# Hyena filters interleaved with the S5 tables in a two-layer hybrid backbone

## The chip, the cores and the metric

The kernel runs on one core of one Trainium2 chip. The metric is device time in microseconds (us), the median of three runs. A core has a matrix engine (TensorE, PE in the rows), a vector engine (VectorE, DVE), a scalar engine (ScalarE, ACT), a general engine (GpSimd, POOL) and a queue engine (SyncE, SP) that here issues nearly all transfers. Each engine works through its own instructions in order; semaphores tie them together.

## The reference, cut to what matters

Two layers act on 256 latent tokens and 256 context tokens. Layer 0, the one concerned, mixes tokens in three parallel branches read from one input projection:

```python
p = modulate(x, shift, scale) @ w_in                  # (L, 6656)
# Hyena: filters are functions of position, then two gated long convolutions
h = sin(freq0 * (z @ w1 + b1)); h = sin(freq1 * (h @ w2 + b2))
h = (h @ w3 + b3) * exp(-tn * abs(decay))             # filters, (L, 2 orders, 2 directions, 512)
z = parts[-1]
for o in range(2):
    z = parts[o] * two_sided_long_conv(z, h[:, o, 0], h[:, o, 1], bias[o])   # by FFT
# Conformer: GLU, depthwise convolution of 31 taps, LayerNorm, swish
# S5: diagonal state space of 64 states in 32 groups of 16 channels, both directions
abar = exp(lam * dt); bbar = (abar - 1) / lam * b
y = Re(C scan(abar, bbar u)) ; y = g * sigmoid(g @ w_glu), g = gelu(y + d * u)
out = (sig(g_hy) * y_hy + sig(g_cf) * y_cf + sig(g_s5) * y_s5) @ w_o
```

A feed-forward network follows, dense in layer 0 and with eight experts in layer 1. Everything is float32.

## The kernel before, in words

A float32 matmul is done as three with the operands split into a high and a low part (`mm3`, L119 to L123); ScalarE casts the high part and VectorE subtracts the low one (`split`, L113 and L114). Weights come as `land` tiles of 128x1024 from the queue SP and are split the same way. The input projection `p` runs in 128x512 tiles.

What depends on the parameters alone is worked out on the chip before it is used, and written as tables to device memory.

- `s5_pre(l)` makes the S5 tables. It has a head (exponentials and sines of all groups) and then four blocks of eight groups. Per block: load `bc`; small products `bb` (L255 to L260); two tiles `cb` made by GpSimd (L265, L268); complex products on VectorE (`cmul`, L277 to L282, tiles `sw` and `tm`); matmuls `kp` (L292, L295), their copy `kt`, the transposes `kq`, the copy `kf`, to which `kd` is added (L306); 15 transfers of `kf` to the table `s5kk` (L309); 16 transposes `tp`, copies `weT` and their transfers (L316 to L318); the same products again on GpSimd (`s5wc`); and sines of the step angles (`tr`, L328 and after).
- `hy_filters(l)` makes the spectra of the long convolutions' filters. Two sine stages (`hp`, L493 and L495; `hid`, L498), then for each of two orders: four tiles `h`, each a matmul times a window `win`, an exponential from ScalarE (L514 to L518); sums and differences `hs` (L526), split into `hh` and `hl`; the transform `kh` of 12 matmuls; its copy `ko` (L534) and the transfer to the table `kd` (L535).

The mixer then uses these: `hy_kk` loads the spectra as `kk` (L609) into the ring "K"; `zc` and `zs` are the forward transforms, products with `kk` follow on VectorE (L581 to L586), `iv` are the inverse ones. `s5_main` has per block `ep`, `yp` (tables `we`, `tb`, `wc`, `mt`), the sum `ya` (L422) and its transposes `yt` (L427). `gl` is the S5 branch's gate, `dc` the conformer's convolution, with taps at L671, a mean taken off at L677 and the variance `va` at L684; `bo` are the branches' output projections.

Tiles live in rings: a ring has a fixed number of buffers under one tag, and its next tile waits for the release of the oldest. The ring of `u2` has four buffers and takes tiles of 128x512; here pass `bc`, `bb`, `cb`, `kf`, `kt` and `kd` of S5 and `win`, `hs` and `ko` of the filters. Ring "K" (taken by `t4(..., "K")`) has two.

The order of instructions on each engine is made when the program is built: a scheduler orders them from the order of the program, priorities, dependences and rings. `self.bg` is a list of generators that `pump` drains, one after the other; in layer 0 first all of `s5_pre(0)`, then all of `hy_filters(0)` (L1458). `both(a, bs)` is a generator that advances `a` one step and then `bs` two.

Of the kernel before, what the change touches and what calls it, by code (L numbers as in the profile page):

```python
# [80 lines left out]
class Net:  # L81
# [392 lines left out]
    def hy_filters(self, l):  # L474

        nc = self.nc
        zT = self.t2([33, 256], "zT")
        nc.sync.dma_start(zT, self.i["zT"])
        w12 = self.t2([64, 2, 64], "w12")
        nc.sync.dma_start(w12[0:33, 0], self.i["hy_f_w1"][l])  # L480
        nc.sync.dma_start(w12[:, 1], self.i["hy_f_w2"][l])
        hc = self.sm.tile([128, 6], FT, name="hc", tag="hc", bufs=1)
        nc.sync.dma_start(hc[0:64, 0:4], self.i["hyc"][l])
        nc.sync.dma_start(hc[:, 4:6], self.i["tn"])
        dft = self.hy_table(self.mx, "dft", tag="U", bufs=self.bufs["U"])
        hid = self.t2([65, 256], "hid")
        ag = self.t2([64, 512], "ag")
        nc.vector.memset(hid[64:65], 1.0)
        a, nn = ag[:, :256], ag[:, 256:]
        for q in range(2):  # L490
            pp = self.ps("hp", "aux")[0:64, 0:256]
            if q == 0:
                nc.tensor.matmul(pp, w12[0:33, 0], zT, start=True, stop=True)  # L493
            else:
                nc.tensor.matmul(pp, w12[:, 1], hid[0:64], start=True, stop=True)  # L495
            nc.vector.tensor_scalar(a, pp, hc[0:64, q:q + 1], hc[0:64, 2 + q:3 + q], op0=OP.add, op1=OP.mult)
            self.reduce2pi(a, nn, (P1, P2, P3))
            nc.scalar.activation(hid[0:64], a, AF.Sin)  # L498
        yield
        for o in range(2):  # L500
            w3 = self.t4([65, 1024], "w3", "U")
            nc.sync.dma_start(w3, self.i["hy_w3a"][l, :, o * 1024:(o + 1) * 1024])
            dec = self.t4([128, 1024], "dec", "U")
            nc.sync.dma_start(dec, self.i["hy_decay"][l:l + 1, o * 1024:(o + 1) * 1024].to_broadcast([128, 1024]))
            nc.vector.scalar_tensor_tensor(dec, dec, -1.0, dec, op0=OP.mult, op1=OP.max)
            bias = self.t2([1, 512], "bias")
            nc.sync.dma_start(bias, self.i["hy_bias"][l, o:o + 1])
            hq = []
            for q in range(2):
                h = self.t4([128, 2, 512], "h", "Y")  # L510
                hq.append(h)
                for tt in range(2):
                    win = self.u2([128, 512], "win")
                    nc.scalar.activation(win, dec[:, q * 512:(q + 1) * 512], AF.Exp, scale=hc[:, 4 + tt:5 + tt])  # L514
                    pp = self.ps("h3", "aux")
                    nc.tensor.matmul(pp, hid[:, tt * 128:(tt + 1) * 128], w3[:, q * 512:(q + 1) * 512],
                                     start=True, stop=True)
                    nc.vector.tensor_mul(h[:, tt], pp, win)  # L518
                yield
            nc.vector.tensor_add(hq[0][0:1, 0], hq[0][0:1, 0], bias)  # L520
            nc.vector.memset(hq[1][0:1, 0], 0.0)
            for r in range(2):
                hh, hl = (self.t4([128, 2, 512], n, "Y", FR) for n in ("hh", "hl"))
                for tt in range(2):
                    hs = self.u2([128, 512], "hs")
                    nc.vector.tensor_tensor(hs, hq[0][:, tt], hq[1][:, tt], op=OP.add if r == 0 else OP.subtract)  # L526
                    self.split(hh[:, tt], hl[:, tt], hs)
                for ft in range(2):
                    ko = self.u2([128, 512], "ko")
                    pp = self.ps("kh", "aux")  # L530
                    c = slice(r * 256 + ft * 128, r * 256 + ft * 128 + 128)
                    for tt in range(2):
                        self.mm3(pp, [t[:, tt, c] for t in dft], (hh[:, tt], hl[:, tt]), tt == 0, tt == 1)
                    nc.scalar.activation(ko, pp, AF.Copy, scale=1.0 / 256.0)  # L534
                    nc.sync.dma_start(self.kd[l][o, r, :, ft], ko)  # L535
                yield
# [867 lines left out]
    def body(self, dbg=None):  # L1404
# [44 lines left out]
        with tc.high_priority():  # L1449
# [5 lines left out]
            for g in m:  # L1455
                self.run(g)
            self.prepare(xr, (0, 1), self.mo[0, 0], self.mo[0, 1])
        self.bg = [self.s5_pre(0), self.hy_filters(0)]  # L1458
        self.pump(1000)
        self.dfs = self.hy_table(self.dftp, "dfs")  # L1460

# [116 lines left out]
```

## Time and profile before

| | |
|---|---|
| runs | 2612.32, 2604.16, 2600.77 us; median 2604.16 |
| profiled execution | 2605.18 us, of it the span of the profile 2603.3 |
| TensorE (matmul) | 2361.7 us busy, 91% |
| VectorE | 2157.8 us, 83% |
| ScalarE | 1373.9 us, 53% |
| GpSimd | 191.6 us, 7% |
| transfers | 229 GB/s over the span |
| mean granted clock of TensorE | 0.943 of full speed |

TensorE is the busiest engine, and most of the span belongs to the feed-forward parts and the experts. The change lies in layer 0's token mixer, roughly the first 500 us. So the page's sums say little; the rows below cut that stretch into windows and then follow single engines through it. In a row of the timeline an instruction's start and duration are followed by engine, line, operation and tiles; in square brackets stands how long the engine had been idle before and what ended that.

### The profile page before, as it was taken

The page shows a single profiled execution, that of the slowest core. Times are in us where ns is not written, and L with a number is a line of the kernel's source. Part 1 is how long each engine was busy: PE and PEld are TensorE (multiplying, and loading weights), DVE is VectorE, ACT ScalarE, POOL GpSimd, SP SyncE. Part 2 cuts the span into 40 slices and gives each one's busy share as a digit, 9 for nine tenths or more (in the row PEclk, how much of TensorE's full clock was granted, in tenths as well). Part 3 has the DMA queues.
Part 4 walks back from the last instruction along what each step waited for, and adds up shares of the span by engine and source line. Part 5 has one row for each costly group of instructions (what it writes and reads, how often), then busy time and mean ns, then how long its engine had stood idle before and what let it go on. Part 6 is the DMA issues. An engine that isn't in the chain of part 4 may idle for free. (4 is left out here: it accounts for less than half of the span.)

```text
span 2603.3 us, 35249 instructions
## 1 busy us (share of the span) xinstructions
PE 2361.7 (91%) x12456; PEld 1935.8 (74%) x12456; DVE 2157.8 (83%) x3182; ACT 1373.9 (53%) x1957; POOL 191.6 (7%) x210
## 2 busy tenths in 40 slices
PE   7958989999899999968869969999999999999986
PEld 2735876788788778748759958888887788878775
DVE  7877899974758988875798678888988889888897
ACT  3434432333543323325435537777877777777775
POOL 1540010000100023230000010000000000000000
PEclk8968999999899999989879979999999999999998
DMA  6546425542235555655535539989999898999985
GB/s 240 190 166 146 137 90 170 194 155 91 80 107 179 182 177 185 208 212 160 162 94 155 178 125 360 347 326 353 352 357 348 324 346 334 354 352 354 351 314 221
DMA packets 170713, 597.26 MB, mean 229 GB/s; under 512 B 59606, under 2 KB 68504, under 8 KB 127520
## 3 DMA queue, kind: packets, MB, share of 16 engines
q1 hardware_dynamic: 170528, 594.94, 65.1%
q8 instruction: 99, 1.62, 0.2%
q14 instruction: 86, 0.70, 0.1%
HBM read 561.87 MB, written 33.00 MB: 229 GB/s over the span
## 5 line engine op out<-in xcount | busy, mean ns | idle before, releaser
L114 DVE TENSOR_TENSOR mwl<-mland,mwh 128x1024 fp32r<-128x1024 f32 x672 | 788.2, 1219 | 78.0 <-ACT mwh L113 65.0
L113 ACT CAST mwh<-mland 128x1024 fp32r<-128x1024 f32 x672 | 675.9, 1052 | 126.9 <-PE mp L123 37.3
L113 ACT CAST wh<-land 128x512 fp32r<-128x512 f32 x396 | 244.9, 621 | 516.0 <-PE p L122 210.7
L114 DVE TENSOR_TENSOR wl<-land,wh 128x512 fp32r<-128x512 f32 x396 | 293.8, 746 | 122.8 <-ACT wh L113 115.6
L123 PE MATMUL p<-hh,wl 128*128 128x256 f32 (+1 forms) x800 | 271.9, 343 | 3.0 <-DVE wl L114 2.9
L121 PE MATMUL p<-hh,wh 128*128 128x256 f32 (+1 forms) x800 | 271.4, 340 | 2.4 <-DVE w L583 1.4
L122 PE MATMUL p<-hl,wh 128*128 128x256 f32 (+1 forms) x800 | 269.9, 338 | 0.1
L1156 PE MATMUL mp<-mwl,xg 128*128 128x512 f32 x560 | 223.9, 402 | 5.4 <-DVE mwl L114 5.3
L1156 PE MATMUL mp<-mwh,xg 128*128 128x512 f32 x560 | 221.9, 398 | 3.2 <-ACT mwh L113 3.0
L121 PE MATMUL mp<-mwh,xg 128*128 128x512 f32 x448 | 177.8, 397 | 2.6 <-ACT mwh L113 2.6
L122 PE MATMUL mp<-mwl,xg 128*128 128x512 f32 x448 | 177.5, 396 | 1.7 <-DVE mwl L114 1.5
L123 PE MATMUL mp<-mwh,xg 128*128 128x512 f32 x448 | 175.9, 393 | 0.0
L789 DVE SCALAR_TENSOR_TENSOR ma<-mw,sv,ma 128x512 f32<-128x512 f32 x196 | 151.6, 793 | 23.5 <-DMA mw<-in_w_mod 23.2
L123 PEld LDWEIGHTS p<-hh,wl 128*128 128x128 f32 x800 | 152.5, 191 | 23.7 <-DVE wl L114 6.9
L121 PEld LDWEIGHTS p<-hh,wh 128*128 128x128 f32 x800 | 152.9, 191 | 20.3 <-issue 1.7
L122 PEld LDWEIGHTS p<-hl,wh 128*128 128x128 f32 x800 | 152.7, 191 | 15.9 <-issue 0.6
L123 PE MATMUL fo<-hh,wl 128*128 128x512 f32 (+1 forms) x384 | 146.7, 383 | 6.6 <-DVE wl L114 6.6
L121 PE MATMUL fo<-hh,wh 128*128 128x512 f32 (+1 forms) x384 | 146.6, 382 | 1.7 <-ACT hh L749 0.9
L122 PE MATMUL fo<-hl,wh 128*128 128x512 f32 (+1 forms) x384 | 145.5, 380 | 0.1
L671 DVE SCALAR_TENSOR_TENSOR dc<-ub,cfp,dc 128x512 f32<-128x512 f32 (+1 forms) x240 | 136.2, 607 | 0.4
L1156 PEld LDWEIGHTS mp<-mwl,xg 128*128 128x128 f32 x560 | 106.9, 191 | 30.4 <-DVE mwl L114 9.8
L1156 PEld LDWEIGHTS mp<-mwh,xg 128*128 128x128 f32 x560 | 107.0, 191 | 24.5 <-ACT mwh L113 4.3
(462 smaller groups left out, 4712.1 us busy)
## 6 DMA issues: line engine op xcount, KB each, us to landing
mland<-in_moe_w SPq DMA_DIRECT2D x336, 1024.0 KB, 6.8
mw<-in_w_mod SPq DMA_DIRECT2D x96, 512.0 KB, 4.2
land<-in_w_in SPq DMA_DIRECT2D x96, 512.0 KB, 3.7
land<-in_ffn_w SPq DMA_DIRECT2D x66, 512.0 KB, 3.5
land<-in_w_bo SPq DMA_DIRECT2D x24, 512.0 KB, 3.6
s5wc<-sw SPq DMA_DIRECT2D x16, 512.0 KB, 5.4
s5we<-weT SPq DMA_DIRECT2D x16, 512.0 KB, 4.5
we<-s5we SPq DMA_DIRECT2D x16, 512.0 KB, 4.2
```

The lines of the kernel that those rows point to most:

```text
L113: nc.scalar.copy(h, src)
L114: nc.vector.tensor_sub(lo, src, h.bitcast(FT))
L121: nc.tensor.matmul(o, a[0], b[0], start=start, stop=False)
L122: nc.tensor.matmul(o, a[0], b[1], start=False, stop=False)
L123: nc.tensor.matmul(o, a[1], b[0], start=False, stop=stop)
L671: nc.vector.scalar_tensor_tensor(d, ub[:, :R, i:i + 64], cfp[:, j, i:i + 1], d, op0=OP.mult, op1=OP.add)
L789: nc.vector.scalar_tensor_tensor(ac[:, t], wk, self.sv[:, k, t:t + 1], ac[:, t], op0=OP.mult, op1=OP.add)
L1156: self.nc.tensor.matmul(o, x[0][:, i], w[r], start=start and r == 0, stop=stop and r == 1)
```

## The change

`hy_filters` gets a helper `tmp` that, in layer 0, takes `win`, `hs` and `ko` from ring "K" instead of ring `u2`; layer 1 keeps `u2`. In the program's order, `hy_filters(0)` and `s5_pre(0)` no longer follow one another: they are passed through `both`, the filters' step first, then two steps of the S5 tables, and so on. From L477 on, the new kernel's line numbers are one higher.

```diff
     def hy_filters(self, l):
...
+        tmp = lambda nm: self.u2([128, 512], nm) if l else self.t4([128, 512], nm, "K")
...
-                    win = self.u2([128, 512], "win")
+                    win = tmp("win")
...
-                    hs = self.u2([128, 512], "hs")
+                    hs = tmp("hs")
...
-                    ko = self.u2([128, 512], "ko")
+                    ko = tmp("ko")
...
-        self.bg = [self.s5_pre(0), self.hy_filters(0)]
+        self.bg = [self.both(self.hy_filters(0), [self.s5_pre(0)])]
```

`both` stands unchanged in the kernel:

```python
    def both(self, a, bs):
        b = itertools.chain(*bs)
        end = object()
        while True:
            x = next(a, end)
            yield
            for _ in range(2):
                y = next(b, end)
                yield
            if x is end and y is end:
                return
```

TensorE shortly after the last p of the first stretch, before: block 3's `kp` and its transposes (`sw` and `cb` are its operands), then the filters' first sine stage `hp`, then the forward transforms `zc` and `zs`.

```order
L295 MATMUL kp_900<-sw_890,cb_882 32x16 x4
L295 MATMUL kp_900<-sw_891,cb_883 32x16 x4
L301 MATMUL kq_935<-ident_110,kt_933 128x128 x2
L316 MATMUL tp_958<-ident_110,sw_890 128x128 x4
L316 MATMUL tp_964<-ident_110,sw_890 128x128 x4
L316 MATMUL tp_972<-ident_110,sw_891 128x128 x4
L316 MATMUL tp_978<-ident_110,sw_891 128x128 x4
L493 MATMUL hp_1026<-zT_1009,w12_1011 64x256
L121 MATMUL zc_2251<-vT0_2216,dfsh_1230 128x512
L121 MATMUL zs_2252<-vT0_2216,dfsh_1230 128x512
```

The same stretch now, shortly after the last p: the end of block 2's `kp`, its transposes, and the filters' second pair of `h` and the `kh` of the second order; block 3's `kp` follows these.

```order
L295 MATMUL kp_909<-sw_881,cb_873 32x16 x4
L295 MATMUL kp_909<-sw_882,cb_874 32x16 x4
L301 MATMUL kq_944<-ident_110,kt_942 128x128 x2
L316 MATMUL tp_967<-ident_110,sw_881 128x128 x4
L316 MATMUL tp_973<-ident_110,sw_881 128x128 x4
L316 MATMUL tp_981<-ident_110,sw_882 128x128 x4
L316 MATMUL tp_987<-ident_110,sw_882 128x128 x4
L517 MATMUL h3_1008<-w3_891,hid_388 128x512
L517 MATMUL h3_1013<-w3_891,hid_388 128x512
L121 MATMUL kh_1070<-hh_1059,dfth_384 128x512
L121 MATMUL kh_1080<-hh_1059,dfth_384 128x512
```

Before, one S5 block stands here and the filters wait behind it; now three blocks (1, 2 and 3) stand behind the last p, with the filters between them, and the sine stages stand earlier, among the p's.

TensorE at the end of the last S5 block, before: the transposes `yt` of block 3 follow the last p of this stretch, and the gate's matmuls `gl` follow them directly.

```order
L122 MATMUL p_3127<-hl_100,wh_3134 128x512
L123 MATMUL p_3127<-hh_99,wl_3135 128x512
L427 MATMUL yt_2194<-ident_110,ya_2188 64x128 x4
L427 MATMUL yt_2203<-ident_110,ya_2188 64x128 x4
L121 MATMUL gl_3200<-gH_3176,wh_3192 128x512
L121 MATMUL gl_3216<-gH_3176,wh_3196 128x512
```

The same place now: the same `yt` stand between matmuls of an earlier tile `p`, and 67 p's come before the first `gl`.

```order
L123 MATMUL p_3013<-hh_99,wl_3021 128x512
L121 MATMUL p_3013<-hh_99,wh_3020 128x512
L427 MATMUL yt_2194<-ident_110,ya_2188 64x128 x4
L427 MATMUL yt_2203<-ident_110,ya_2188 64x128 x4
L122 MATMUL p_3013<-hl_100,wh_3020 128x512
L123 MATMUL p_3013<-hh_99,wl_3021 128x512
```

`yt` moved forward past 77 p's, of which 67 now lie between it and `gl`.

SP, the queue of transfers, around the first load of the spectra `kk`, before: two pairs of `ko`'s writes, each followed by a load, and then the S5 inputs `U`.

```order
L535 DMA kd0_95<-ko_1087 128x512
L535 DMA kd0_95<-ko_1097 128x512
L609 DMA kk_2212<-kd0_95 128x1024
L535 DMA kd0_95<-ko_1117 128x512
L535 DMA kd0_95<-ko_1127 128x512
L609 DMA kk_2213<-kd0_95 128x1024
L352 DMA U_1698<-s5u0_86 16x16x64 x3
```

SP now, from the last block's `kf` (15 transfers) on; the first `kk` comes after these, a `tb`, two `wc`, eight `mt`, one more `we` and eight more `mt`.

```order
L536 DMA kd0_95<-ko_1069 128x512
L536 DMA kd0_95<-ko_1079 128x512
L322 DMA s5wc0_82<-sw_1174 128x1024
L309 DMA s5kk0_83<-kf_1056 16x8x16 x15
L318 DMA s5we0_81<-weT_1146 128x1024
L318 DMA s5we0_81<-weT_1160 128x1024
L322 DMA s5wc0_82<-sw_1175 128x1024
L536 DMA kd0_95<-ko_1195 128x512
L536 DMA kd0_95<-ko_1205 128x512
L332 DMA s5tb0_84<-tr_1215 128x1024
L364 DMA we_1716<-s5we0_81 128x1024
L364 DMA we_1718<-s5we0_81 128x1024
```

The first `kk` moved from behind the first pair of `ko`'s writes to behind the last pair and behind loads of the S5 tables.

## Rows read from the trace of the kernel before

**Rows 1.** Windows: stretch, its us; busy us (instructions) of PE, PEld, DVE, ACT, POOL; PEclk, DMA.

```profile
0.00:137.00 137.00, 116.96 (x628) 72.83 (x629) 116.04 (x222) 54.49 (x96) 52.66 (x47) 0.95 0.62 212
137.00:168.00 31.00, 11.96 (x119) 9.64 (x118) 23.51 (x29) 10.53 (x19) 20.41 (x14) 0.61 0.31 100
168.00:200.00 32.00, 23.13 (x48) 12.43 (x47) 19.19 (x36) 10.26 (x19) 0.90 (x1) 0.63 0.61 212
200.00:250.00 50.00, 39.66 (x190) 27.37 (x191) 38.13 (x61) 22.31 (x39) 0.56 (x5) 0.86 0.66 135
250.00:375.00 125.00, 121.69 (x743) 101.64 (x742) 105.19 (x166) 51.30 (x84) 7.77 (x24) 1.00 0.44 133
375.00:400.00 25.00, 15.91 (x57) 12.34 (x56) 25.00 (x37) 9.43 (x14) 1.20 (x3) 0.80 0.11 32
385.00:395.00 10.00, 8.14 (x23) 6.17 (x24) 10.00 (x14) 3.23 (x4) 0.00 (x0) 0.66 0.21 66
400.00:500.00 100.00, 98.34 (x403) 68.73 (x402) 99.07 (x159) 30.17 (x52) 0.00 (x0) 1.00 0.59 196
```

**Rows 2.** Timeline of PE: start, us, engine, line, operation, tiles, [idle before <- releaser].

```profile
66.14 0.42 PE L292 MATMUL kp<-sw,cb 128*32 128x128 f32 x8
...
136.74 0.39 PE L121 MATMUL p<-hh,wh 128*128 128x512 f32 x1
136.96 0.39 PE L122 MATMUL p<-hl,wh 128*128 128x512 f32 x1
...
157.90 0.65 PE L292 MATMUL kp<-sw,cb 128*32 128x128 f32 x8 [5.13 <-DVE sw L282]
...
180.49 0.39 PE L123 MATMUL zs<-vT,dfsl 128*128 128x512 f32 x1
...
224.75 0.40 PE L123 MATMUL kh<-hh,dftl 128*128 128x512 f32 x1
...
227.71 3.68 PE L373 MATMUL ep<-U,we 128*128 128x64 f32 x32
...
249.48 0.73 PE L121 MATMUL iv<-yh,dfsh 128*128 128x512 f32 x2
...
379.83 3.46 PE L427 MATMUL yt<-ident,ya 128*64 128x128 f32 x16 [4.56 <-DVE ya L422]
385.17 0.96 PE L121 MATMUL gl<-gH,wh 128*128 128x512 f32 x3 [1.88 <-ACT gH L452]
...
561.14 0.50 PE L684 MATMUL va<-ones,sq 128*128 128x1 f32 x4
```

**Rows 3.** Timeline of DVE, the same columns.

```profile
140.66 2.43 DVE L306 TENSOR_TENSOR kf<-kf,kd 128x128 f32<-128x128 f32 x1
...
162.59 2.00 DVE L306 TENSOR_TENSOR kf<-kf,kd 128x128 f32<-128x128 f32 x1
...
205.00 0.69 DVE L581 TENSOR_TENSOR w<-zc,kk 128x512 f32<-128x512 f32 x1 [3.60 <-DMA kk<-kd]
...
517.54 2.47 DVE L677 TENSOR_TENSOR dc<-dc,mu 128x512 f32<-128x512 f32 x4
```

**Rows 4.** The page: GB/s in forty slices of the span, and the weights' splits.

```profile
GB/s 240 190 166 146 137 90 170 194 155 91 80 107 179 182 177 185 208 212 160 162 94 155 178 125 360 347 326 353 352 357 348 324 346 334 354 352 354 351 314 221
...
L114 DVE TENSOR_TENSOR wl<-land,wh 128x512 fp32r<-128x512 f32 x396 | 293.8, 746 | 122.8 <-ACT wh L113 115.6
```

**Rows 5.** One line (L671): engine, operation, tiles, count: duration ns min/median/max, starts, forms.

```profile
L671 DVE SCALAR_TENSOR_TENSOR dc<-ub,cfp,dc x120: 722/739/755, 335.4 to 510.6; 128x512 f32<-128x512 f32 x120
```

**Rows 6.** Timeline of ACT, the columns of the other timelines.

```profile
172.53 0.72 ACT L514 ACTIVATE win<-dec,hc 128x512 f32<-128x512 f32 x1 [2.49 <-DMA s5kk<-kf]
```

**Rows 7.** One tile (ko): its transfers.

```profile
DMA to landing us min/median/max: 2.1/2.2/2.2
```

**Rows 8.** Groups of ACT by line, 0 to 260 us.

```profile
L514 ACT ACT_TABLE_LOAD x2 | 2.6, 1283 | 0.0
```

**Rows 9.** Timeline of POOL, the same columns.

```profile
150.47 0.71 POOL L265 MEMSET cb<- 128x384 f32 x1 [6.23 <-DMA s5kk<-kf]
```

## Prediction

> **What bounds the kernel now.** I read the windows first, because an average over the whole span hides the stage that the change touches. In the token mixer of layer 0 (the first 500 us) TensorE is nearly full, except in two places [rows 1]. From 137 to 250 us it is busy for 11.96 + 23.13 + 39.66 = 74.8 of 113 us, at granted clocks of 0.61, 0.63 and 0.86. From 375 to 400 us it is busy for 15.91 of 25 us at 0.80. Elsewhere (250 to 375, 400 to 500) it is at 97% or more and at a clock of 1.00. The second reading is VectorE in the same rows: 116 of 137 us at first, 80.8 of 113 us in the gap, then 105 of 125, and full from 375 to 500 us. So VectorE does not fill the gap either: it idles 32 us there. The gap is a chain of waits between engines.
>
> Third, TensorE's own order [rows 2]. The first 288 matmuls "p" of the input projection end at 137 us, 0.22 to 0.23 us apart. The state-space (S5) tables begin inside them: block 0's kp at 66.1. But kp of block 3 comes at 157.9, after the last p, and the Hyena filters only behind it; their last kh is at 224.8. After them come ep of S5 block 0 (227.7) and the end of the first stage of the Hyena branch (the iv at 249.5, where p's begin again). Between 137 and 250 us TensorE has hardly any ready work. Fourth, the waits in the brackets of the same rows. Block 3's kp waited 5.1 us for VectorE's sw; a later pair makes the bubble at 375 to 400: yt on ya (4.56) and gl on gH (1.88), with gl on gL right behind.
>
> **The change, part by part.** It has two edits: who goes first, and which ring the filters' three passing tiles use. The arithmetic, and so the busy work, stays the same; what can change is idle time and time at half clock. Between 137 and 250 us these are 38.2 us idle and, at the clocks above, 11.96 x 0.39 + 23.13 x 0.37 + 39.66 x 0.14 = 18.8 us of busy time lost. Between 375 and 400 us they are 9.1 us idle and, from the row of 385 to 395 us, 10 x 0.34 = 3.4 us.
>
> *The filters move forward, the S5 tables back.* In the new order the filters' two sine stages, the four h of the first order and the first twelve kh stand among the 288 p's, where TensorE has work in any case. Block 0's kp goes from behind 2 (its first four matmuls) and 26 p's to behind 156: about 100 us at 0.23 us each. Blocks 1, 2 and 3 all come behind the last p; before, only block 3 did. What enters the p stretch (about 1 us of hp, 1 of h, 12 x 0.23 = 2.8 of kh) is about what leaves it (kp, kq and tp of two blocks), so I put its end at 140, 2 us later than now.
>
> *The tail behind the last p.* Before, one S5 block and nearly all the filter work stood there. Now three blocks and about half of the filter work do, interleaved. The step from one block's kf to the next kp is 157.9 - 143.1 = 14.8 us [rows 2, 3], and kp to kf adds 6.7 (162.59 + 2.0 - 157.9). Together 21.5 us. I take 19 us for the first step, part of whose vector work still lies under the p's, and 25 for the second, which has six of the filters' h, hs and hl among it, some 4.5 us at the 0.746 us of a split [rows 4]: kp of block 1 at 141, of 2 at 160, of 3 at 185, its kf at 192. The last kh then is at about 198, where the old one ended at 225. That is the gain of this part: 57 us of filter chain no longer follow the S5 chain, and 27 us of S5 chain are added. The first transforms (zc), which before stood between the two hp, end at 209 instead of 180.5, and ep of block 0 starts at 211 instead of 227.7.
>
> *What is late next.* The kernel spectra kk. Before, VectorE's first product with kk began at 205.0, after waiting 3.6 us for that load [rows 3]. Now the loads stand on SP behind the last pairs of ko's writes, three we, one tb, two wc and sixteen mt loads. Those are 4 MB, 12 us at 360 GB/s, the highest slice of the page [rows 4]. From the last ko at about 203, and with 3 to 6 us for kk itself, I expect kk at 219 to 221; its products, splits and iv follow until about 237. So at the second iv (249.5 before) both kernels stand at the same clock time. But in the new one S5 block 0 is done to its yt and block 1 to its ep, which before came behind that iv: 3.7 us for an ep and 3.5 at most for a yt [rows 2], less a little since that yt ran beside a falling clock, 6.5 us of TensorE. VectorE has 11 us of such work behind it. This part is worth 6.5 us; were kk there when zc ends, 10 us sooner, it would be 16.
>
> *The bubble at 375 to 400 us.* Before, yt of the last S5 block has no p left behind it: gl follows directly, and TensorE waits for ya, gH and gL. Now 67 p's stand between yt and gl, 67 x 0.23 = 15 us. VectorE also reaches that block's ya with 22 of the taps of the conformer's convolution (L671) fewer in front of it (10 instead of 32, 0.739 us each [rows 5], 16.3 us) and nine of the weights' splits fewer (L114, 0.746 us [rows 4], 6.7 us). So its result is there when TensorE comes, and the 9.1 + 3.4 = 12.5 us can all go. But VectorE is full from 375 to 500 us, and the taps put off must still be done. The term is between 0 and 12.5. Their deadline is L677 (517.5) and its reader va (561.1) [rows 2, 3]: 43 us of room, more than 16.3, so the taps themselves cost nothing. I take 5 of the 12.5, under half, because the stretch behind it has VectorE at 99 of 100 us and TensorE can only run ahead as far as VectorE delivers splits.
>
> *The ring.* win, hs and ko leave the ring u2 (four buffers, where the S5 blocks' bc, bb, cb, kf, kt and kd pass) for K (two buffers). This keeps the filters from waiting on kf's writes, as a win did for 2.5 us before [rows 6], and S5 from waiting on theirs. In exchange a tile of K waits for the one two before it; if that is a ko, for its write, 2.2 us to landing [rows 7]. Since ko follows its own twelve kh, I cost this at nothing; its bounds are -2.5 and, where a write stands behind a block's kf group on SP, the price of the slower rival below.
>
> *Table loads.* ScalarE's exponentials (win) and sines now alternate: seven table loads up to the first S5 output instead of four, 3 x 1.283 = 3.9 us [rows 8]. ScalarE is busy 97.6 of the first 250 us [rows 1], so I cost this at nothing; with no cover at all it is 3.9 us.
> The Trainium skill (page "ScalarE: Activation LUTs", section "Table sets: the hidden batching unit") has a rule that speaks against the change: do all calls of one table set together. Its section "What ACT_TABLE_LOAD costs" gives about 1283 ns for the load, as the row does, and 1380 ns of drain, which no row here shows; by it the three loads would be an estimated 8 us, and the sum -3.5 if nothing covered them.
>
> Sum: -6.5 - 5 + 0 + 0 = -11.5 against the profiled execution's 2605.2 us (span 2603.3), which lies 1.0 above the median of the runs, 2604.16: about 2593.5. The ends: -16 - 12.5 - 2.5 = -31, and +3.9 with the first two terms at nothing; beyond that only the slower rival reaches.
>
> **The rivals.** *A larger gain.* The whole bubble goes (12.5) and kk is early enough to give about 12 of the 16: 2605.2 - 24.5 = 2580.5. For it: 67 p's are more than the 9.1 us of idle time they must cover, and TensorE's clock stays up when nothing empties it (before, gl matmuls ran at 0.66 after the waits [rows 1]). Against: VectorE is full behind it.
>
> *No change.* S5 starts 34 us later, and ep waits for its last tables. If the first step takes 25 us as well, kp of block 3 comes at 191, and ep and kk 6 us later, which eats the first term; and if VectorE, full anyway, sets the pace behind 375 us, the bubble only moves behind the p's: 2605.2 - 0.5 - 0, about 2604.5. For it: block 3 took 21.5 us before, with little of the filters' vector work in it. Against: in the new order VectorE has less in front of ya.
>
> *Slower: the two K buffers against SP's queue.* In the new order the pairs of ko's writes of the second and later halves stand behind a block's fifteen kf writes. Such a group kept POOL waiting 6.2 us, from kf's end at 143.1 to 150.47 [rows 3, 9], 7.4 us in all. A K tile that follows is held until its ko is written, and behind it, in program order, wait the S5 products on VectorE or the sines on ScalarE. It can happen at three pairs, 3 x 7.4 = 22 us on the chain that is now the longest, so 2605.2 - 11.5 + 22 = 2616. It decides from about 11.5 us of such stalls, two groups, since that eats the whole sum. For it: VectorE and ScalarE work in order, and a kf group did hold POOL. Against: ko follows its block's kf by the time of twelve kh, so that its write seldom meets a full queue.
>
> *The change does nothing.* Excluded: the order of all engines differs for about the first 690 us.
>
> **How the numbers follow.** Forecast 0.46, larger gain 0.20, no change 0.18, slower 0.16. Half a per cent, 13 us, is about what a measurement here can tell from no change (the three runs of before span 2600.8 to 2612.3): faster means under 2591.1, slower above 2617.2. The forecast's own range is 2584 to 2602; about 0.37 of it lies under 2591. Faster: 0.20 x 0.95 + 0.46 x 0.37 = 0.36. Slower: half of its case, 0.08, and 0.05 from the upper edge of no change, 0.13. Same: the remaining 0.51. The range from 2574 to 2616 leaves out one in ten at either side: the far end of the large gain, and the upper half of the slower case.
>
> **What would show it.** Right: the windows of 137 to 250 us hold more TensorE time, the last kh is near 200 and ep of block 0 near 211; the first product with kk waits, longer than 3.6 us; yt, gl and their waits vanish from the list, and 385 to 395 us is at full clock. Wrong: kp of block 3 later than 195; POOL, ScalarE or VectorE waiting for "kd<-ko"; win or hs in the list of waits; or a new wait of bo or va behind 400 us, which would show the gain given back to VectorE.

## The result and the profile after

| | before | after |
|---|---|---|
| median of the runs, one comparison | 2604.97 us | 2622.35 us |
| span of the profiled execution | 2603.3 us | 2630.4 us |
| TensorE busy | 2361.7 us | 2368.6 us |
| first matmul behind the mixer (`rb`, after `va`) | 576.2 us | 591.5 us |
| first matmul of the feed-forward part (`fo`) | 703.2 us | 725.1 us |

The changed kernel is slower: ratio 1.0060, 95% interval 1.0044 to 1.0077, about 16 us (the medians of four runs each lie 17.4 us apart; the text goes by the ratio). The forecast was 2593.5 and its range ended at 2616. The profiled execution of after took 2632.2 us, 10 more than its own median, so its span is not taken for the loss. But its token mixer shows where time went: `rb`, behind all of it, begins 15.3 us later, about the loss by the ratio. At `fo` the shift is 22 us and at the last expert matmul `mp` 24 (2598.7 instead of 2574.9), more than the loss, in an execution that was itself above its median.

Windows of after, the columns and stretches of [rows 1]:

```profile
0.00:137.00 137.00, 116.45 (x487) 69.55 (x488) 110.52 (x217) 58.22 (x97) 36.97 (x37) 0.94 0.55 192
137.00:168.00 31.00, 17.41 (x135) 12.36 (x133) 26.90 (x38) 11.18 (x20) 12.44 (x10) 0.83 0.47 149
168.00:200.00 32.00, 16.58 (x168) 12.13 (x168) 23.04 (x33) 11.22 (x20) 21.70 (x14) 0.63 0.54 144
200.00:250.00 50.00, 22.99 (x97) 18.33 (x99) 27.25 (x37) 14.72 (x27) 7.61 (x8) 0.62 0.66 203
250.00:375.00 125.00, 115.78 (x730) 97.66 (x729) 96.93 (x155) 51.47 (x85) 5.07 (x20) 0.95 0.38 112
375.00:400.00 25.00, 25.00 (x118) 20.56 (x118) 23.21 (x34) 11.95 (x18) 3.59 (x5) 1.00 0.32 95
385.00:395.00 10.00, 10.00 (x45) 8.29 (x45) 8.72 (x14) 7.67 (x10) 0.00 (x0) 1.00 0.57 180
400.00:500.00 100.00, 97.80 (x396) 68.80 (x395) 99.71 (x160) 29.89 (x52) 3.31 (x2) 1.00 0.54 179
```

The bubble at 375 to 400 us is gone: TensorE is busy for 25.00 of 25 us at full clock, where [rows 1] had 15.91 at 0.80. But from 137 to 250 us it does less, 17.41 + 16.58 + 22.99 = 57.0 us instead of 74.8, and most of the difference lies in the last stretch: 22.99 against 39.66. From 250 to 375 another 5.9 us are missing. VectorE has not taken the place: in 200 to 250 it is busy for 27.25 of 50 us, before for 38.13.

TensorE in after, to be held against [rows 2]:

```profile
147.81 0.64 PE L292 MATMUL kp<-sw,cb 128*32 128x128 f32 x16
...
195.90 0.64 PE L292 MATMUL kp<-sw,cb 128*32 128x128 f32 x16 [0.31 <-ACT ko L535]
...
211.74 0.55 PE L123 MATMUL kh<-hh,dftl 128*128 128x512 f32 x1
...
217.35 0.39 PE L123 MATMUL zs<-vT,dfsl 128*128 128x512 f32 x1
224.09 7.06 PE L373 MATMUL ep<-U,we 128*128 128x64 f32 x32 [6.35 <-issue]
...
247.82 0.70 PE L415 MATMUL yp<-wc,sp 128*64 128x128 f32 x4 [12.84 <-ACT sp L407]
...
275.30 0.73 PE L121 MATMUL iv<-yh,dfsh 128*128 128x512 f32 x2 [2.96 <-ACT yh L113]
...
383.12 1.09 PE L427 MATMUL yt<-ident,ya 128*64 128x128 f32 x8
...
400.33 0.39 PE L121 MATMUL gl<-gH,wh 128*128 128x512 f32 x1
...
575.61 0.50 PE L685 MATMUL va<-ones,sq 128*128 128x1 f32 x4
```

Up to the last `kh` the new order is ahead: 211.7 instead of 224.8. Then it turns. After the transforms (217.35) TensorE has, until 247.8, only `ep`, 7.06 us long where it took 3.68, and one group of `yp`; the two longest waits there are 6.35 and 12.84 us. The iv before which the p's start again is at 275.3, 26 us later than before. What is late is seen on SP and VectorE.

The queue SP in after (start, us taken to issue, transfers):

```profile
200.97 12.37 SPq L309 DMA_DIRECT2D s5kk<-kf  x15
...
215.22 2.40 SPq L536 DMA_DIRECT2D kd<-ko  x2
...
221.92 9.64 SPq L382 DMA_DIRECT2D mt<-s5kk  x8
231.77 0.34 SPq L364 DMA_DIRECT2D we<-s5we  x1
232.20 3.85 SPq L382 DMA_DIRECT2D mt<-s5kk  x8
236.24 1.25 SPq L610 DMA_DIRECT2D kk<-kd  x1
237.59 0.38 SPq L364 DMA_DIRECT2D we<-s5we  x1
238.01 0.43 SPq L610 DMA_DIRECT2D kk<-kd  x1
```

VectorE in after:

```profile
198.36 1.53 DVE L527 TENSOR_TENSOR hs<-h 128x512 f32<-128x512 f32 x1 [5.33 <-DMA kd<-ko]
200.28 2.05 DVE L527 TENSOR_TENSOR hs<-h 128x512 f32<-128x512 f32 x1 [0.39 <-DMA kd<-ko]
202.24 2.11 DVE L304 TENSOR_TENSOR kd<-s5k,lag 128x128 f32<-128x128 f32 x1
...
204.88 2.45 DVE L306 TENSOR_TENSOR kf<-kf,kd 128x128 f32<-128x128 f32 x1
...
240.83 0.69 DVE L582 TENSOR_TENSOR w<-zc,kk 128x512 f32<-128x512 f32 x1 [3.09 <-DMA kk<-kd]
```

The first product with `kk` starts at 240.83, where [rows 3] had 205.00. Its load leaves SP at 236.24, behind the last pair of `ko`'s writes. Before, the same load was issued ahead of the second order's filters:

```profile
201.68 0.32 SPq L609 DMA_DIRECT2D kk<-kd  x1
```

It could be, because ring K then held none of the filters' tiles. Now win, hs and ko pass through ring K until the last `ko` is written, and `kk` takes both of its buffers. Once the last `ko`'s writes are issued (217.62), `kk` still takes 18.6 us to its turn on SP, most of them behind the sixteen `mt`.

### The profile page after: what moved, and what is told of

Same layout as the page of the kernel before. It is cut to its first block, busy times and chain, and to the rows that moved or that the text cites. A ratio compares the mean times of both kernels' runs of the same rounds, so it can differ in the third digit from the quotient of the medians.

```text
span 2630.4 us, 35240 instructions
## 1 busy us (share of the span) xinstructions
PE 2368.6 (90%) x12456; PEld 1950.6 (74%) x12456; DVE 2160.5 (82%) x3182; ACT 1376.2 (52%) x1961; POOL 199.1 (8%) x210
```

## The experiments

Each ratio is against runs of the kernel before on the same chip, with its 95% interval. Diffs show the lines put in, against the changed kernel unless the kernel before is named. "±" at a difference of two ratios joins their intervals. Three theories were open at first: the spectra's ring (kk shares ring K with the filters), the S5 tables that come late (three blocks behind the last p), and the prediction's own slower rival, waits for `ko`'s write in a ring of two. Later, VectorE's pace was asked as well.

**The two halves of the change alone.** The order without the ring, then the ring without the order:

```diff
+        tmp = lambda nm: self.u2([128, 512], nm)
```


> Only the interleaving is kept; win, hs and ko stay in the ring u2 of four buffers. On TensorE three S5 blocks still come behind the last p (first kp behind 156 p's). Theory: the loss of the changed kernel (+17 us) is mostly made by the two buffers of K, whose reuse waited 7.9 us (ScalarE's win) and 6.5 us (VectorE's hs) for writes of ko. Without them those waits go, kp of block 3 comes near 183 us instead of 196, and the time is 2604 to 2611. Rival: the place of the S5 chain behind the p's and the late kk cost it, whatever the ring; then this stays at 2617 to 2625, or is above it, since S5 and the filters now share four buffers.

```diff
+        self.bg = [self.s5_pre(0), self.hy_filters(0)]
```


> Only the ring is changed: first all S5 tables and then the filters in the program's order, as before, but win, hs and ko in ring K. The order on TensorE is then not that of before: the filters' h and kh come among the p's and all four blocks' kp behind the last p. Theory that the S5 chain behind the p's is what costs: this is the worst, four blocks of about 20 us from 140 on, ep of block 0 near 235, 2620 to 2640. Theory that only the waits for ko's writes cost: the filters are done before any kf is written, no wait for ko's writes of more than 2 us, 2604 to 2612.

Order only: 2659.12 us, 1.0194 (1.0175 to 1.0212). Ring only: 2620.16, 1.0043 (1.0028 to 1.0058). In ring u2 the interleaved filters and the S5 tables hold each other up; a row of its list of waits, 0 to 260 us (in total, times, longest):

```profile
PE kp L292 <- DVE h L519: 27.1, 1, 27.1
```

So the interleaved order needs another ring. But the ring alone, at the old order, costs 11 us, and in that kernel the filters' last `kh` is about where it was (227.3 instead of 224.8). The expectation had misread its order: blocks 2 and 3 have their kp at 121.4 and 151.8, as in before (122.7 and 152.1), not behind the last p. So its time at the edge of the first theory's range is luck and says nothing on late S5 tables. What moved is the product with the spectra:

```profile
244.61 0.69 DVE L582 TENSOR_TENSOR w<-zc,kk 128x512 f32<-128x512 f32 x1 [2.77 <-DMA kk<-kd]
```

**The waits for ko's write.** Once with win, hs and ko as halves of K's tiles, which makes four small buffers of two large ones; once with ko's writes issued by ScalarE:

```diff
...
+            t = self.t4([128, 2, 512], nm, "K")
+            return [t[:, 0], t[:, 1]]
...
```


> The changed kernel, with the K ring's buffers used as pairs: the two win of an h, the two hs of a half and the two ko of a half are the two halves of one buffer, so that a ring of two buffers holds four of the small tiles and hs comes two tiles after a ko, not one. The order on TensorE stays that of the changed kernel to a few p's. Theory of the two K buffers: the waits of 7.9 and 5.3 us for ko's writes go or fall under 3 us each, kp of block 2 is at 162 and of block 3 near 184, and the time falls by 8 to 13 us to 2608 to 2614. Rival (S5 chain and kk behind it on SP): within 4 us of the changed kernel, 2617 to 2625.

```diff
+                    (nc.sync if l else nc.scalar).dma_start(self.kd[l][o, r, :, ft], ko)
```


> The changed kernel, with layer 0's writes of ko issued from ScalarE's own queue, so that they no longer stand behind the fifteen writes of kf on SP. Theory of SP's queue: the write lands 2.2 us after its ko, the waits of win and hs for it fall from 14.4 us in all to under 5, kp of block 3 comes near 186 instead of 196. But behind it the order differs too: here gl follows yt directly again, so the bubble of 10 us near 380 can come back. 2605 to 2615. Rival (the two buffers themselves, or the S5 chain): waits stay over 10 us, 2617 to 2628.

2626.27 us, 1.0065 (1.0050 to 1.0080), and 2626.32, 1.0060 (1.0044 to 1.0077). Both remove the waits for `kd<-ko` in the first 260 us, in after 7.88 us on ScalarE's table load and 6.5 us on VectorE's hs, and neither gains anything: block 3's kp, expected near 184 and 186, starts at 199.3 and 195.7, and the first product with kk at 240.6 and 241.8. The prediction's slower rival named a real wait, and it is not the cause.

**The spectra on another queue.** In after, kk's loads are issued by ScalarE:

```diff
+            (self.nc.sync if l else self.nc.scalar).dma_start(k[r], self.kd[l][o, r])
```


> The changed kernel with layer 0's loads of the spectra kk issued from ScalarE's queue, past the sixteen mt loads on SP. In the changed kernel the first kk was issued at 236 us and VectorE's first product with it began at 240.8. Theory of the late kk: it comes at 218 to 225, iv starts near 237 instead of 253, VectorE's idle time up to 400 us falls from 92 to about 80, and the time falls by 8 to 12 us to 2610 to 2615. Rival: S5's own chain (ep at 224, its scan, sp and yp until 253) holds VectorE and TensorE in that stretch anyway, and the time stays at 2618 to 2626.

2619.26 us, 1.0036 (1.0024 to 1.0048). The first product moves from 240.8 to 231.6. Passing SP's `mt` loads thus gives back about 9 us of the delay and about 6 us of time (difference of the ratios 0.0024 ± 0.0021); the loads still wait for the last `ko`.

**S5 and filters with other weights in turn.** One S5 step, then two filter steps:

```diff
+        self.bg = [self.both(self.s5_pre(0), [self.hy_filters(0)])]
```


> The interleaving turned round: one step of the S5 tables, then two of the filters; the ring K as in the change. TensorE's first kp then stands behind 34 p's instead of 156 and the filters' h and kh still among the p's, with one or two S5 blocks behind the last p. Theory that the number of S5 blocks behind the last p sets VectorE's idle time, at 20 to 27 us a block: the first ep or iv comes 15 to 25 us sooner than in the changed kernel, VectorE's idle time to 400 us is under 75, and the time is 2590 to 2605. Rival (the ring K and the mixing itself cost): 2612 to 2625.

2628.27 us, 1.0073 (1.0057 to 1.0089). The expectation misread the order: block 0's kp stands behind 194 p's here, so S5 is still later than in after (ep at 239), not earlier. What the run does show is a second way to be late. The filters are done early (last kh 166.8), kk is issued at 187.7, and no product waits for it. But block 3's first kp starts only at 213.7, VectorE's time up to 233 goes mostly to that block, and the first product, behind that work, starts at 233.6. S5 tables as late as that go with a loss of 19 us without any wait for kk.

**VectorE's pace.** 20 of the 120 taps of layer 0's conformer convolution are left out of the computation, 20 x 0.739 = 14.8 us [rows 5], in after and in before:

```diff
+            for i in range(1, 26 if l == 0 else 31):
```


> The changed kernel without 20 of the 120 taps of layer 0's convolution in the conformer (five of each channel tile; left out of the sum): 20 x 0.74 = 14.8 us less work for VectorE behind 335 us, the order before it the same. VectorE is full from 400 to 587 us in the changed kernel, and in all kernels so far the end of the mixer (the matmul rb behind va) came at VectorE's busy time plus its idle time until then. Theory that VectorE sets the pace there and that its idle time in the first 400 us (92 against 73 us) is the loss: rb moves forward by 12 to 15 us, from 591.5 to about 578, the time falls to 2604 to 2612, about that of the kernel before. Rival that TensorE's waits before 300 us are what ends late: the time stays at 2617 to 2625.

> The kernel before without the same 20 taps (left out of the sum). Its VectorE is idle 12.5 us between 400 and 576 us, and TensorE full from 400 to 560. Theory that VectorE sets the pace in the changed kernel but shares it with TensorE before: a gain, but a smaller one than in the changed kernel, 2 to 9 us, 2597 to 2605; the difference between the two kernels without these taps shrinks from 17 to about 8 us. Rival: both gain the same 12 to 15 us (VectorE is the bound in both), or neither.

2619.43 us, 1.0041 (1.0025 to 1.0057), and 2607.91, 1.0000 (0.9988 to 1.0011). Against after the first is 0.0019 ± 0.0023, no difference to be told, though the interval alone leaves room for a part of the 14.8 us. The end of the mixer decides: `rb` begins at 590.0 instead of 591.5 in after and at 574.3 instead of 576.2 in before, 1.5 and 1.9 us sooner where 12 to 15 were expected. So VectorE, at 99% from 400 to 500 us in both kernels, does not set the time there.

**One tile in ring K.** The kernel before, with only the very last `ko` of layer 0 taken from K:

```diff
+                    ko = self.t4([128, 512], "ko", "K") if l == 0 and o + r + ft == 3 else self.u2([128, 512], "ko")
```


> The kernel before with one tile moved: the last of the eight ko takes its buffer from ring K instead of u2, all other tiles stay. The loads kk take the two buffers of K as well, behind the filters in the program's order, so the first kk must then wait until that last ko has been written; on SP it stands behind all of ko's writes. S5 tables and filters keep their places on TensorE. Theory that the ring K costs through kk: the first product with kk comes at 230 to 245 instead of 205, the first iv at 240 or later instead of 222, rb at 582 to 592 instead of 576, and the time is 2612 to 2620, like that with only the ring changed (+11). Rival, that the filter tiles' own waits (hs for ko's writes, 8.4 and 4.3 us there) cost: no change, 2602 to 2609.

2619.46 us, 1.0033 (1.0019 to 1.0047). Nothing else was changed, the filters and S5 stand within 2.5 us of before (block 3's kp at 153.6, the last kh at 222.4), and one tile of 128x512 makes it slower by 9 us. VectorE there:

```profile
237.94 0.69 DVE L581 TENSOR_TENSOR w<-zc,kk 128x512 f32<-128x512 f32 x1 [0.96 <-DMA kk<-kd]
```

**Ring K for the first order of the filters only.** kk then waits for the first order's last ko alone; the second order is in u2. With S5 first, with the change's order, and with four S5 steps and one filter step in turn (the lines of the last; the other two have the first line and their own order):

```diff
+        tmp = lambda nm: self.u2([128, 512], nm) if l or o else self.t4([128, 512], nm, "K")
...
+        def turn(a, b, n):
+            live = [True, True]
+            while any(live):
+                for _ in range(n):
+                    live[0] = next(a, self) is not self
+                    yield
+                live[1] = next(b, self) is not self
+                yield
+
+        self.bg = [turn(self.s5_pre(0), self.hy_filters(0), 4)]
```


> The program's order of before (all S5 tables, then the filters), ring K for the tiles of the first order's filters, u2 for those of the second. Against the kernel with only the ring changed this only frees K before the second order. Theory of kk's buffer: kk is loaded near 205 as in the kernel before, rb is at 574 to 578, the time 2602 to 2609, equal to before. Rival, that K's two buffers cost the filters themselves: 2613 to 2620, as with the ring alone.

> The changed kernel with ring K for the filters of the first order only; win, hs and ko of the second order take u2, as before. K is then free early and on SP kk stands right behind ko's writes of the first order. Theory that kk's buffer is the loss: the first product with kk is near 215 instead of 241, and the time falls to 2605 to 2613 in spite of some waits in u2. Rival, that S5 blocks 2 and 3 and the filters of the second order, which now share u2, stall each other as in the kernel with the interleaving alone (27 us): 2630 to 2655.

> A version meant to be better than both: four steps of the S5 tables, then one of the filters, and ring K for the first order's tiles only. On TensorE the kp stand behind 2, 143, 230 and 288 p's (before 2, 122, 232, 288), the sine stages and the first two h among the p's; kk right behind ko's writes of the first order. Theory (S5 early, K free early): the last kp stays near 160, the first kh comes near 175 instead of 193, iv near 212, VectorE's idle time up to 400 us is 60 to 68 instead of 73 us, and the time is 2592 to 2602. Rival, that filters among the S5 blocks delay these by as much: 2603 to 2612.

S5 first: 2614.86 us, 1.0016 (0.9999 to 1.0032), the product at 211.7. That is 0.0027 ± 0.0022 under the ring alone, 7 of its 11 us, and cannot be told from before. The change's order: 2635.88, 1.0098 (1.0076 to 1.0121); ring u2 holds the second order up: ScalarE's hh waits 27.6 us for an hs. Four to one: 2599.05, 0.9950 (0.9933 to 0.9967), faster than both kernels. In it block 3's kp starts at 162 instead of 196, the last kh is at 211, and kk is loaded in time:

```profile
210.67 0.69 DVE L582 TENSOR_TENSOR w<-zc,kk 128x512 f32<-128x512 f32 x1 [1.63 <-DMA kk<-kd]
```

**Ring and order apart.** After this the ring's share in the changed kernel itself had been seen only together with other edits. So win, hs and ko were moved to ring "s2", four tiles of 128x512 that the filters' own zT, w12, hid and bias use, which leaves K to kk; with each of the three orders, and beside them four to one with everything in K:

```diff
+        tmp = lambda nm: (self.t2 if l == 0 else self.u2)([128, 512], nm)
```


> The changed kernel, but the filters' passing tiles win, hs and ko take the ring of four small tiles that zT, w12, hid and bias use, instead of ring K; so ring K belongs to the spectra kk alone and the first pair of kk can be loaded as soon as its own ko are written. Theory (the loss is the spectra's ring plus the later S5 tables): kk is issued before 215 us, the first product with kk starts before 222 (240.8 in the changed kernel), and the time falls by 8 to 12 us to 2608-2614, ratio to before 1.001-1.004. Rival (the S5 tables behind the last p cost it all): kk comes earlier and the time stays, 2620-2626, ratio 1.005-1.008.

> Four S5 steps and then one filter step in turn (as in the fast version), but with the filters' tiles of both orders in ring K. Theory: kk waits for the last ko again, the first product with kk moves from 211 to 230-240 us, and the fast version's time of 2599 grows by 9-11 us to 2608-2611, ratio 1.000-1.002. Rival (the order alone made the fast version): 2597-2602, ratio 0.994-0.997.

> Four S5 steps and one filter step in turn, with win, hs and ko of both orders in the ring of four small tiles. Theory: kk is as early as in the fast version (product at 205-212 us) and no filter tile waits in ring u2 or K, so 2594-2600, ratio 0.993-0.996. Rival (room in rings beyond kk's does not matter, or that ring is too narrow): 2599-2606, ratio 0.995-0.998.

> The old order, all S5 tables and then the filters, with win, hs and ko in the ring of four small tiles. With ring K this order took 2620. Theory: with kk's ring free the first product with kk is back at 205-212 us and the time at 2604-2609, ratio 0.999-1.001. Rival (what ring K cost this order lay in the filters' own waits and not in kk): 2615-2620.

| order | ring u2 | ring K | K, first order only | ring s2 |
|---|---|---|---|---|
| S5, then filters | 1 (before) | 1.0043 | 1.0016 | 1.0050 (1.0031 to 1.0068) |
| the change's | 1.0194 | 1.0060 (after) | 1.0098 | 0.9997 (0.9986 to 1.0008) |
| four S5, one filter | | 1.0022 (1.0013 to 1.0032) | 0.9950 | 0.9947 (0.9929 to 0.9965) |

In the change's order (2607.52 us) the free ring K takes back 0.0063 ± 0.0020, 16 us: the whole loss. In the four to one order (2614.66 and 2592.78) it makes 0.0075 ± 0.0020, 20 us, more than expected. The last is the fastest kernel of this study. The changed kernel with K free, VectorE, and two of its windows:

```profile
215.62 0.69 DVE L582 TENSOR_TENSOR w<-zc,kk 128x512 f32<-128x512 f32 x1 [3.65 <-PE zc L123]
```

```profile
200.00:250.00 50.00, 34.78 (x173) 26.95 (x172) 40.92 (x57) 18.19 (x32) 8.89 (x9) 0.85 0.60 182
375.00:400.00 25.00, 17.24 (x63) 12.94 (x61) 25.00 (x37) 9.06 (x13) 1.99 (x5) 0.73 0.15 47
```

kk is issued at 149.5 and 165.7, and the product waits for `zc` now, not for kk. Block 3's kp (195.4), the last zs (217.5) and ep (223.9) stand where they stood in after, and ScalarE's table load still waits 6.7 us for `kd<-ko`. VectorE's hs wait less for `kd<-ko` (1.1 us instead of 6.5) and the last kh is earlier (203.1 instead of 211.7), but neither brought zs or ep forward, and taking such waits away alone gained nothing above. What differs behind them is kk, and TensorE has 34.78 us of work in 200 to 250 instead of 22.99; `rb` begins at 577.6, 1.4 us behind before. So with K free the change's order, late S5 tables and early filters together, costs nothing against before and gains nothing. Four to one with K free is faster than it by 0.0050 ± 0.0021, 13 us; of these, 5 are there at `rb` (572.5). The second window has the bubble of before again.

S5 first with ring s2 did not do what was expected (2620.63 us). kk is early there too (203.1), but the products' own tiles `w` come from ring s2, and so they stand behind the `ko` in it:

```profile
226.67 0.69 DVE L583 TENSOR_TENSOR w<-zs,kk 128x512 f32<-128x512 f32 x1 [2.92 <-DMA kd<-ko]
```

It is the same fault in another ring: the transforms' next user shares a ring with the filters' passing tiles. Here the filters still run (last kh 225) when the first products are due (205 before, 223 now). In the four to one order with ring s2 the first product, expected at 205 to 212, waits 3.4 us for a `ko` as well and starts at 221.9, later than in the changed kernel with K free, and that kernel is fast all the same. So the time of this product does not order all kernels, and why the wait costs so much more here was not followed up.

## Why the prediction was wrong

**The step that failed is "The ring", costed at nothing.** It listed the waits among win, hs and ko, and the wait for ko's write, and took ring K for a ring that had no other user then. But the prediction's own account of the mixer has `kk` in it, and its paragraph on what is late next set kk behind the last `ko` without seeing why: the ring, not only the order of SP, put it there. So a part of the ring's price stood in the sum unnamed: a late kk is why the tail was put at 6.5 and not at 16. That part was too small. The last pair of ko's writes left SP at 215.2, where the last ko was put at 203, and the first kk 21 us behind it, where 12 were allowed. Measured by itself the ring is 16 us in the change's order (0.0063 ± 0.0020), 11 in the old one. With K free kk is there when zc ends, for which the working gives -16 for the tail and -5 for the bubble; the kernel is at 0.9997, within 4 us of before. So these two terms did not come either.

**"Worth 6.5 us", the tail behind the last p.** The first step was the end of the p's: 147 instead of 140; what held them up by these 7 us was not followed. The first kp, at 101.3, came as forecast. From there block 1's kp came at 147.8 (141 forecast), block 3's at 195.9 (185), the last kh at 211.7 (198), zs at 217.4 (209), ep at 224.1 (211). The steps between blocks, about 21 and 27 us, were longer than the 19 and 25 taken by 2 us each; the other 7 are the p's. All that was left of the head start was 3.6 us of ep, and kk at 240.8 instead of 219 to 221 made it a loss of 17.8 us of TensorE's work between 137 and 250 us. Slips of the working that change nothing in this: 140 lies 3 us behind the old end of the p's, not 2; the large gain comes to 2580.7; and the kp at 157.9 is the second half of block 3's, whose first half starts at 152.1.

Part of these steps' length is VectorE beside GpSimd, though no run takes that part alone. GpSimd in after, while VectorE has the rows from 198 to 207 us above:

```profile
196.99 2.34 POOL L279 TENSOR_TENSOR sw<-sw,tm 128x1024 f32<-128x1024 f32 x1
199.41 2.36 POOL L281 TENSOR_TENSOR tm<-ari,bc 128x1024 f32<-128x1024 f32 x1
201.74 2.47 POOL L280 TENSOR_TENSOR sw<-ari,bb 128x1024 f32<-128x1024 f32 x1
204.28 2.89 POOL L282 TENSOR_TENSOR sw<-sw,tm 128x1024 f32<-128x1024 f32 x1
```

VectorE's rows end at 199.89, 202.33, 204.35 and 207.33, each 0.1 to 0.6 us behind the end of a GpSimd product (199.33, 201.77, 204.21, 207.17); the L306 takes 2.45 us, and 0.28 at its shortest in this kernel. The Trainium skill (page "SBUF — State Buffer", section "SBUF: two separate sides") says that a VectorE operation with two inputs in SBUF, the memory of the tiles, and a GpSimd operation that reads it take a shared pair of ports in turn, each for a whole instruction; the trace agrees, with the ends above. By it an hs of the filters or a kf of S5 beside GpSimd's products waits for the product that runs. That three blocks behind the p's have less to cover this with is argued, not measured.

**"The bubble at 375 to 400 us", 0 to 12.5, taken as 5.** The bubble went in full: 9.1 us idle became 0 and the clock 0.80 became 1.00. But the p's that fill it were there because 17.8 + 5.9 us of TensorE's work had been put off before it. With K free these p's are done earlier, no p stands between yt and gl, and the bubble is back (17.24 of 25 us); and in the kernel before with one ko in K, with 9 us lost, it is filled as well (25.00). It was no gain of its own, and the sum counted a postponement as one. In the four to one order it is filled as well (24.69 of 25 us with ring s2) but with TensorE's sum to 400 us at 331.5 against 329.3 before, so nothing had been put off there.

**"No change" through VectorE.** It was not the pace: 14.8 us less of its work moved the end of the mixer by under 2 us. **Table loads**, costed at nothing: not contradicted. With K free the changed kernel has seven in the first 250 us instead of four, and the time of before; no run takes the loads alone. **The slower rival** had the right sign and nearly the size (2616), by luck, with the wrong place: the wait of a ring was the cause, not of K's small tiles for one another but of kk for them. Its chance of 0.16 weighed the size of a wait and not who else uses the ring.

What stays open: the fastest kernel is 14 us under before, and its profiled execution shows 3.3 us of that at the first `fo` (699.9) and about 10 at the last `mp` (2565.3); what is added behind `fo` lies in parts that the edits do not touch. Single profiled executions differ by as much (after's lay 10 us above its median), so where the rest arises was not shown.

## What to carry to other kernels

Before moving passing tiles to another ring, list every other taker of that ring and when its next tile is due: a ring sets an order between tiles that have nothing else to do with each other, and one tile in the wrong ring cost 9 us here. A bubble that fills with work put off earlier is no gain; judge a change of order by a milestone behind all of it, such as the first matmul of the next stage, and by the time itself. When two chains are interleaved, try the weights: of the orders tried here only the one that kept the longer chain ahead, four steps to one, was faster than before.

## What the hardware showed that was not expected

A small operation of VectorE beside GpSimd's 128x1024 products took nearly nine times as long (2.45 instead of 0.28 us) and ended just behind a GpSimd product. And `ep`, 32 matmuls, took 7.06 us in after, where it took 3.68 us in [rows 2]. In after the granted clock over these matmuls (224 to 231 us) is 0.50, the lower of the two levels, 1.2 GHz, and TensorE had been without work for 6.35 us; before it is 1.00 (227.7 to 231.4 us), right behind the last kh. Here the engine that ran dry paid again when work came.
